# Weight work of the down projections in one chain per engine, and new orders of their units

## The chip, the core and the metric

The kernel runs on one core of a Trainium2 chip. The metric is device time in microseconds from start to end of one execution, the median of several. TensorE (PE) multiplies, VectorE (DVE) does elementwise work, ScalarE (ACT) does casts and activations, GpSimd (POOL) does a little arithmetic and some stores, and SyncE (SP) issues nearly all loads.

## What is computed

One encoder layer on 256 tokens of width 2048 in float32: two feed-forward blocks around a mixer (a gated recurrence and windowed attention). The change is in the feed-forward blocks, which run twice with other weights:

```python
def swiglu(x, w_gate_up, w_down):          # (256,2048) (2048,11264) (5632,2048)
    gate, up = jnp.split(x @ w_gate_up, 2, axis=-1)
    return (jax.nn.silu(gate) * up) @ w_down

ff = swiglu(rms_norm(x, pre_norm_ffn1[layer]), w_ffn1_gate_up[layer], w_ffn1_down[layer])
x = x + 0.5 * rms_norm(ff, post_norm_ffn1[layer])
```

## The kernel before

**Three products for one.** To keep float32 accuracy every matrix is split into a rounded part h and a remainder l (both fp32r), and a product is h·h + h·l + l·h. For weights this split is made on the fly: `split_act` casts on ScalarE (L191) and subtracts on VectorE (L192). `split_half` does it for half of a loaded tile (128x1024) and takes one of five h and one of five l buffers.

**Units.** A feed-forward block first has 11 gate-up groups of 512 columns (class `Gated`, 8 units each), then the down projection (class `Pairs`): 22 units of 256 rows of `w_down`, in two runs of 1024 output columns each. A unit's weights are 128x2048 floats, loaded in two halves of 512 KB into one of four places (`raw0` to `raw2` and a part of the tile `rooms`).

**Plain and mixed.** A plain unit (`plain`) is 8 products, 24 matmuls. A mixed unit (`seven`) uses Strassen's scheme: of the 2x2 blocks b11, b12, b21, b22 of its weights it makes sums on VectorE, and needs 7 products, 21 matmuls. Its weight work, in the order of the code: the split of b11 into ha and la; the split of the lower half (`lower`); the sum at L480 (128x1024, in place); the sums at L483 and L484 (128x512, in place); the split of the upper half (`upper`), which needs L480; the split of the lower half again (`third`), which needs L484. TensorE uses them in the order b11, lower, upper, third. The left operand of a mixed unit is a tile of sums too. For the down stages these are made once, in the gate-up stage (`units`: copy L968, sums L403 to L407, split), stored to DRAM by GpSimd (L978, tile `ss`) and read back in each run (L608, tile `sp`, 512 KB, four buffers). `MIXED` lists which of the 22 units are mixed: 0, 2, ..., 16, 20 and 21.

**The fold.** Four of the seven products add up in four banks `p` over all mixed units of a run, the rest in the four output banks `c`. When the last mixed unit and one plain unit behind it are done, `fold` (L524 to L532: one copy on ScalarE, eight additions on VectorE) adds `p` into `c`.

**Order.** Each engine runs its own queue in the order in which it was filled. That order comes from a planner at build time: it takes the instructions as traced, with priority to the earlier, and issues what its own estimate has ready. `tc.issue_after(ins)` adds a bound for it: what is traced in the block goes behind `ins` if it is on the same engine. It makes no engine wait for another. In `split_half` a bound of this kind holds splits behind `last["sums"]`, which `Gated` sets at L484 and `Pairs` does not (`AHEAD` is true there). With `AHEAD`, `seven` takes `begin_next` as `aside`: its first call loads the next plain unit's weights behind this unit's, its second splits the first half of them, between `upper` and `third`. The orders of the units in the two runs are written out by hand at L1012. In `finish` the last two units of the second run are held: their splits are made first and their products ordered by output bank, with the norm's work between.

Of the kernel before, what the change touches and what calls it, by code (L numbers as in the profile page):

```python
# [11 lines left out]
F32 = mybir.dt.float32  # L12
# [5 lines left out]
ALU = mybir.AluOpType  # L18
AX = mybir.AxisListType

P = 128
# [16 lines left out]
def hymba_layer_kernel(  # L38
# [25 lines left out]
    nc = tc.nc  # L64
# [11 lines left out]
    def nm(s):  # L76
        uid[0] += 1
        return f"{s}_{uid[0]}"

    def pa():  # L80
        return psum.tile([P, 512], F32, tag="pa", name=nm("pa"))

    def pb():
        return psum.tile([P, 512], F32, tag="pb", name=nm("pb"))
# [64 lines left out]
    def load(src, between=None):  # L149
        raw = new_raw()  # L150
        if len(src.shape) == 4:

            dst = raw.rearrange("p (a n b) -> p a n b", a=src.shape[1], n=src.shape[2])
            parts = [(dst[:, a], src[:, a]) for a in range(src.shape[1])]
        else:
            n = src.shape[1]
            dst = raw.rearrange("p (a b) -> p a b", a=n)
            parts = [(dst, src)]
            if n == 2:
                parts = [(dst[:, a], src[:, a]) for a in range(2)]  # L160
        for i, (to, of) in enumerate(parts):
            if i and between:
                between()
            nc.sync.dma_start(to, of)
        return raw

    def split_load(src, hp=hip, lp=lop, between=None, middle=None):
        return split(load(src, between), hp, lp, middle)

    def split(raw, hp=hip, lp=lop, middle=None):  # L170
        hs, ls = [], []
        for i in range(2):
            if i and middle:
                middle()
            h, l = split_half(raw, i, hp, lp)
            hs.append(h)
            ls.append(l)
        return hs, ls

    def split_half(raw, i, hp=hip, lp=lop):  # L180
        part = raw[:, i * 1024 : (i + 1) * 1024]
        h = hp.tile([P, 1024], F32R, tag="h", name=nm("h"))
        l = lp.tile([P, 1024], F32R, tag="l", name=nm("l"))
        with ExitStack() as queued:
            if "sums" in last:
                queued.enter_context(tc.issue_after(last["sums"].ins))
            split_act(h, l, part)
        return h, l

    def split_act(hi, lo, src):  # L190
        nc.scalar.copy(hi, src)  # L191
        nc.vector.tensor_tensor(lo, src, hi.bitcast(F32), ALU.subtract)  # L192


    def rsqrt_of(ssq, scale, eps):
# [17 lines left out]
    def close_far():  # L213
        far["cm"].__exit__(None, None, None)
# [15 lines left out]
    last = {}  # L230
# [114 lines left out]
    class LeadN:  # L345


        def __init__(self, w, c0, slot):
            self.w, self.c0, self.slot = w, c0, slot
# [60 lines left out]
    class Blocks:  # L410
# [1 line left out]

        AHEAD = False
        ahead = between = None

        def __init__(self, tiles, sums):
# [50 lines left out]
        def seven(self, u, aside=None):  # L469

            self.left_early(u)
            raw = load(self.source(u))
            if aside:
                aside()
            b11, b12, b21, b22 = (raw[:, i * 512 : (i + 1) * 512] for i in range(4))
            four = raw.rearrange("p (i c) -> p i c", i=4)
            h, l = self.one_block()
            split_act(h, l, b11)
            lower = split_half(raw, 1)
            nc.vector.tensor_tensor(  # L480
                four[:, 0:2], four[:, 0::3], four[:, 1:2].to_broadcast([P, 2, 512]), ALU.add
            )
            nc.vector.tensor_tensor(b22, b11, b22, ALU.add)  # L483
            sums = nc.vector.tensor_tensor(b21, b22, b21, ALU.add)  # L484
            if not self.AHEAD:
                last["sums"] = sums
            upper = split_half(raw, 0)
            if aside:
                aside()
            third = split_half(raw, 1)  # L490
            if not self.p:
                self.p = [pa(), pa(), pb(), pb()]
            a, w = self.tiles[u], self.left_sums(u)

            def lhs(k, m):
                return [a[:, k, i, m * P : (m + 1) * P] for i in range(2)]

            def summed(j):
                return [w[:, j, i, :] for i in range(2)]

            def rhs(two, n):
                return [x[:, n * 512 : (n + 1) * 512] for x in two]

            for at, left, right in (
                (("p", 0), lhs(0, 0), (h, l)),
                (("c", 0, 0), lhs(1, 0), rhs(lower, 0)),
                (("c", 0, 1), summed(S4), rhs(lower, 1)),
                (("p", 1), summed(S1), rhs(upper, 0)),
                (("p", 3), summed(S3), rhs(upper, 1)),
                (("p", 2), summed(S2), rhs(third, 1)),  # L510
                (("c", 1, 0), lhs(1, 1), rhs(third, 0)),
            ):
                self.three(at, *left, *right)
# [26 lines left out]

        def work(self, upto):

            while self.pos < upto:
                u = self.order[self.pos]
                if u in self.some:
                    v = self.order[self.pos + 1]
                    if self.AHEAD and v not in self.some and self.pos + 1 < upto:
                        self.ahead = [v]
                        self.seven(u, self.begin_next)
                    else:  # L550
                        self.seven(u)
                else:
                    if self.ahead:
                        _, raw, h, l = self.ahead
                        self.ahead = None
                        hs, ls = zip((h, l), split_half(raw, 1))
                    else:
                        hs, ls = split_load(self.source(u))
                    if self.pos == self.after + 1:
                        self.fold()  # L560
                    places = [(k, m, n) for k in range(2) for m in range(2) for n in range(2)]
                    if self.pos in (self.after, self.after + 1):

                        places.sort(key=lambda at: at[1:])
                    for i, (k, m, n) in enumerate(places):
                        if i == 4 and self.between:
                            self.between()
                            self.between = None
                        self.plain(u, hs, ls, m, n, k)
                self.pos += 1  # L570

    class Pairs(Blocks):

# [3 lines left out]
        HELD = 2  # L577
        AHEAD = True

        def __init__(self, w, orders, tiles, sums, room, gain_src, stored=False):  # L580

            super().__init__(tiles, sums)
            self.stored, self.left = stored, {}
            self.w, self.orders = w, orders
            self.room, self.post, self.gain_src = room, None, gain_src
            self.ssq = [
                stat.tile([P, 4], F32, tag="ssqr", name=nm("ssqr"), bufs=2) for _ in range(2)
            ]
            self.y = {}
            open_far(2)  # L590
            self.run(0)
# [73 lines left out]
        def finish(self, mul, post, new_x=None, gain=None, lead=None):  # L665
# [4 lines left out]
            self.post = post  # L670
            self.work(n_order - self.HELD)
            held = []
            for u in order[n_order - self.HELD :]:
                held.append((u, *split_load(self.source(u), hp=post, lp=post)))
            close_far()
            self.half_gain(post)
            raw_places[:] = [r for r in raw_places if r in own_raws]
# [172 lines left out]
    LATE = 8  # L850

    MIXED_IN = (1, 3, 5)
    MIXED = (*range(0, 18, 2), 20, 21)

    def pair_of(xt, u):
        return xt[u // 4][:, u % 4 * 2 : u % 4 * 2 + 2]
# [45 lines left out]
    def ffn(gated, w_dn, post_gain, again, gain=None, lead=None, aside=None):  # L902

        with ExitStack() as st:
# [4 lines left out]
            hts, sums = [], {}  # L909
# [33 lines left out]
            def units(c, scale):  # L943
# [19 lines left out]
                for bank in turned:  # L963
                    g = len(hts)
                    u = bank.rearrange("p (k t) -> p k t", k=2)
                    if g in MIXED:
                        u = room_for("z").rearrange("p (k t) -> p k t", k=2)
# [4 lines left out]
                    hts.append(ht)  # L972
                    if g in MIXED:
                        ws = sums_of(u, room_for("s").rearrange("p (j t) -> p j t", j=4))
# [8 lines left out]
            for g in range(NG):  # L983
# [26 lines left out]
                next(waiting)  # L1010
            close_far()
            orders = [  # L1012
                [1, 3, 0, 5, 2, 7, 4, 9, 6, 11, 8, 10, 13, 12, 15, 14, 16, 17, 20, 21, 18, 19],

                [1, 0, 3, 2, 4, 5, 6, 7, 8, 14, 9, 10, 11, 12, 16, 13, 20, 21, 15, 17, 18, 19],
            ]
            sums.update((u, None) for u in MIXED if u not in sums)
            rows = Pairs(w_dn, orders, hts, sums, work, post_gain, stored=True)
# [18 lines left out]
    with tc.manual_schedule():  # L1037
# [12 lines left out]
        def arrive(i):  # L1050
            nc.sync.dma_start(raw[:, i * 512 : (i + 1) * 512], first[:, i // 2, i % 2])

        h, l = (
            p.tile([P, 1024], F32R, tag=t, name=nm(t)) for p, t in ((hip, "h"), (lop, "l"))
        )
# [89 lines left out]
    def again_from(src):  # L1145
# [15 lines left out]
        aside=other_vectors,  # L1161
# [447 lines left out]
```

## Time and profile before

| | us |
|---|---|
| median of 3 runs | 1841.77 |
| lowest and highest | 1840.83, 1844.27 |
| the profiled execution | 1845.24 |
| its span, first to last instruction | 1843.5 |
| TensorE busy in the span | 1825.4 (99%) |
| VectorE busy | 1641.9 (89%) |
| ScalarE busy | 1106.1 (60%) |

In the profile a line number names the instruction's place in the kernel; L191 and L192 are in the helper `split_act`, so the tile's name tells whose split it is (h and l of a half, ha and la of b11, ht of the left operand). PE is TensorE's matmuls, PEld its weight loads. A row of the timeline has start, duration, engine, line, operation, output <- inputs, and in square brackets how long the engine had been idle before and what it waited for. A row of the waits has the total in us, how often, and the longest. The first down stage runs from about 488 to 702 us of the span, the second from about 1610 to 1826.

### The profile page before, as it was taken

What the parts mean: (1) busy time and instruction counts of PE and PEld (TensorE: products, weight loads), DVE (VectorE), ACT (ScalarE), POOL (GpSimd) and SP (SyncE); (2) the same over time, 40 slices, a digit from 0 to 9 for tenths busy, and PEclk for the clock granted to TensorE, in tenths of its full rate; (3) what the DMA queues carried; (4) which work ended last, traced back from release to release, by engine and by line L of the source; (5) the groups of instructions that cost most, each with busy time, mean ns of one, the idle gap of its engine ahead of it and who ended that gap; (6) DMA issues with size and microseconds to landing.
All of it is one profiled execution on the core that took longest, in us unless ns stands there. A gap on an engine that the chain in (4) does not pass through costs nothing.

```text
span 1843.5 us, 23937 instructions
## 1 busy us (share of the span) xinstructions
PE 1825.4 (99%) x8604; PEld 1519.5 (82%) x8604; DVE 1641.9 (89%) x2076; ACT 1106.1 (60%) x1470; POOL 33.2 (2%) x61
## 2 busy tenths in 40 slices
PE   9999999999999999999999999999999999999998
PEld 7888888888887787888888888888888888887786
DVE  7999999999999998477778798899999999999997
ACT  6555556555555556477678566555655555555553
POOL 1000000000000000000000000000000000000000
PEclk9999999999999999999999999999999999999999
DMA  8566666666877776655555565566666665787774
GB/s 287 195 223 219 198 196 216 215 207 207 288 264 263 239 244 212 218 179 172 163 172 165 178 223 185 197 234 212 207 218 224 212 201 194 254 275 254 244 265 169
DMA packets 192056, 400.45 MB, mean 217 GB/s; under 512 B 11976, under 2 KB 59168, under 8 KB 191168
## 3 DMA queue, kind: packets, MB, share of 16 engines
q1 hardware_dynamic: 188416, 387.24, 63.1%
q0 software_dynamic: 3520, 11.67, 1.6%
q8 instruction: 67, 1.10, 0.2%
q14 instruction: 53, 0.43, 0.1%
HBM read 383.12 MB, written 15.75 MB: 216 GB/s over the span
## 4 chain that ended last, share of the span: by engine, by line
PE 75%; DVE 14%; issue 4%; DMA 4%; ACT 3%; POOL 0%; SPq 0%; DVEq 0%; ACTq 0%; POOLq 0%
PE pa L447 29%; PE pb L447 27%; PE pa L322 8%; DVE l L192 8%; PE pa L327 4%; ACT h L191 2%; DMA raw<-in_w_mix_out_dram 1%; DMA raw<-in_w_ffn_down_dram 1%; DVE raw L480 1%; PE pa L377 1%; PE pa L376 1%; PE pa L375 1%; DVE raw L483 1%; DVE raw L484 1%; DVE la L192 1%
## 5 line engine op out<-in xcount | busy, mean ns | idle before, releaser
L191 ACT CAST h<-raw 128x1024 fp32r<-128x1024 f32 (+1 forms) x691 | 680.7, 1014 | 445.1 <-DVE raw L484 146.9
L192 DVE TENSOR_TENSOR l<-raw,h 128x1024 fp32r<-128x1024 f32 (+1 forms) x691 | 796.4, 1173 | 83.7 <-ACT h L191 43.2
L447 PE MATMUL pa<-h,xt 128*128 128x512 f32 x1176 | 406.2, 392 | 0.0
L447 PE MATMUL pb<-h,xt 128*128 128x512 f32 x1060 | 368.8, 390 | 0.0
L447 PEld LDWEIGHTS pa<-h,xt 128*128 128x128 f32 x1176 | 221.1, 188 | 45.0
L447 PEld LDWEIGHTS pb<-h,xt 128*128 128x128 f32 x1060 | 199.0, 188 | 41.3
L447 PE MATMUL pa<-l,xt 128*128 128x512 f32 x588 | 229.4, 390 | 0.1
L447 PE MATMUL pb<-l,xt 128*128 128x512 f32 x530 | 206.4, 389 | 0.0
L191 ACT CAST h<-rooms 128x1024 fp32r<-128x1024 f32 x138 | 142.3, 1049 | 86.0 <-DVE rooms L484 41.1
L192 DVE TENSOR_TENSOR l<-rooms,h 128x1024 fp32r<-128x1024 f32 x138 | 166.1, 1221 | 28.5 <-ACT h L191 28.2
L322 PE MATMUL pa<-xt,h 128*128 128x512 f32 x672 | 164.7, 394 | 0.0
L447 PE MATMUL pa<-h,ht 128*128 128x512 f32 x440 | 156.2, 391 | 2.2 <-DVE pa L526 2.1
L447 PE MATMUL pb<-h,ht 128*128 128x512 f32 x440 | 155.8, 390 | 0.4 <-DVE pb L530 0.4
L322 PEld LDWEIGHTS pa<-xt,h 128*128 128x128 f32 x672 | 123.0, 188 | 23.6
L447 PEld LDWEIGHTS pa<-l,xt 128*128 128x128 f32 x588 | 110.6, 188 | 22.8 <-DVE l L192 0.8
L447 PEld LDWEIGHTS pb<-l,xt 128*128 128x128 f32 x530 | 99.6, 188 | 20.6
L480 DVE TENSOR_TENSOR raw<-raw 128x1024 f32<-128x1024 f32 x92 | 112.1, 1219 | 1.0
L447 PEld LDWEIGHTS pa<-h,ht 128*128 128x128 f32 x440 | 82.6, 188 | 21.5 <-issue 2.8
L447 PEld LDWEIGHTS pb<-h,ht 128*128 128x128 f32 x440 | 82.6, 188 | 18.4 <-DVE pb L530 1.2
L327 PE MATMUL pa<-xt,l 128*128 128x256 f32 x672 | 91.8, 286 | 0.0
L327 PEld LDWEIGHTS pa<-xt,l 128*128 128x128 f32 x672 | 87.1, 191 | 3.2
L447 PE MATMUL pa<-l,ht 128*128 128x512 f32 x220 | 85.8, 390 | 0.0
(280 smaller groups left out, 2477.5 us busy)
## 6 DMA issues: line engine op xcount, KB each, us to landing
raw<-in_w_ffn_gate_up_dram SPq DMA_DIRECT2D x270, 512.0 KB, 5.0
raw<-in_w_ffn_down_dram SPq DMA_DIRECT2D x132, 512.0 KB, 5.4
raw<-in_w_mix_in_dram SPq DMA_DIRECT2D x52, 1024.0 KB, 4.9
rooms<-in_w_ffn_gate_up_dram SPq DMA_DIRECT2D x80, 512.0 KB, 5.1
rooms<-in_w_ffn_down_dram SPq DMA_DIRECT2D x44, 512.0 KB, 4.8
sp<-ss SPq DMA_DIRECT2D x44, 512.0 KB, 6.6
raw<-in_w_mix_out_dram SPq DMA_DIRECT2D x32, 512.0 KB, 5.3
ss<-rooms POOLq DMA_DIRECT2D x22, 512.0 KB, 3.3
```

The lines of the kernel that those rows point to most:

```text
L191: nc.scalar.copy(hi, src)
L192: nc.vector.tensor_tensor(lo, src, hi.bitcast(F32), ALU.subtract)
L322: nc.tensor.matmul(slot[f], weights(hs, kk, f), xcol(xt, k), start=(k == 0), stop=(k == KT - 1))
L327: nc.tensor.matmul(slot[f][:, 0:T], weights(ls, kk, f), xcol(xt, kh * 8 + kk, 0), start=False, stop=False,)
L375: nc.tensor.matmul(dst, xh, h[:, o : o + n], start=(k == 0), stop=False)
L376: nc.tensor.matmul(dst, xh, l[:, o : o + n], start=False, stop=False)
L377: nc.tensor.matmul(dst, xl, h[:, o : o + n], start=False, stop=(k == KT - 1))
L447: nc.tensor.matmul(self.bank(at), lhs, rhs, start=(n == 1), stop=n in (ends, self.of[at]), skip_group_check=n > ends,)
L480: nc.vector.tensor_tensor(four[:, 0:2], four[:, 0::3], four[:, 1:2].to_broadcast([P, 2, 512]), ALU.add)
L483: nc.vector.tensor_tensor(b22, b11, b22, ALU.add)
L484: sums = nc.vector.tensor_tensor(b21, b22, b21, ALU.add)
```

## The change

A function `chained` is added. While `chain["on"]` is set it places what it makes behind the last piece of chained work on VectorE and behind the last chained cast on ScalarE. `work` sets it for a `Pairs` object with stored sums, which is the case in the two down stages alone (the flag `CHAIN`), and `finish` sets it for the held splits. Every split of a weight half, the split of b11 and the three sums go through it, so that in the down stages all weight work stands on each of the two engines in the order in which it is traced. The second call of `aside` moves from between `upper` and `third` to behind `third`. Even units from 0 to 20 are mixed now: unit 18 comes in, unit 21 goes out, and there are 11 as before. The two orders of units are new. As plain (P) and mixed (M), the first run was P P M P M P M P M P M M P M P M M P M M P P and is P P M P M M P M P M M P M P M M P M P M P P; the second has P M P M M P M P M M P M P M M P M M P P P P in both.

```diff
     def split_half(raw, i, hp=hip, lp=lop):
         ...
+        if chain["on"]:
+            chained(split_act, h, l, part)
+            return h, l
         with ExitStack() as queued:
         ...
+    chain = {"on": False, "at": None}
+
+    def chained(make, *a):
+
+        with ExitStack() as queued:
+            if chain["on"]:
+                for at in ("at", "cast"):
+                    if chain.get(at):
+                        queued.enter_context(tc.issue_after(chain[at].ins))
+            chain["at"] = make(*a)
+            if make is split_act:
+                chain["cast"] = last["cast"]
+        return chain["at"]
+
     def split_act(hi, lo, src):
-        nc.scalar.copy(hi, src)
-        nc.vector.tensor_tensor(lo, src, hi.bitcast(F32), ALU.subtract)
+        last["cast"] = nc.scalar.copy(hi, src)
+        return nc.vector.tensor_tensor(lo, src, hi.bitcast(F32), ALU.subtract)
 ...
-            split_act(h, l, b11)
+            add = nc.vector.tensor_tensor
+            twice = four[:, 1:2].to_broadcast([P, 2, 512])
+            chained(split_act, h, l, b11)
             lower = split_half(raw, 1)
-            nc.vector.tensor_tensor(
-                four[:, 0:2], four[:, 0::3], four[:, 1:2].to_broadcast([P, 2, 512]), ALU.add
-            )
-            nc.vector.tensor_tensor(b22, b11, b22, ALU.add)
-            sums = nc.vector.tensor_tensor(b21, b22, b21, ALU.add)
+            chained(add, four[:, 0:2], four[:, 0::3], twice, ALU.add)
+            chained(add, b22, b11, b22, ALU.add)
+            sums = chained(add, b21, b22, b21, ALU.add)
             if not self.AHEAD:
                 last["sums"] = sums
             upper = split_half(raw, 0)
-            if aside:
+            if aside and not self.CHAIN:
                 aside()
             third = split_half(raw, 1)
+            if aside and self.CHAIN:
+                aside()
 ...
         def work(self, upto):
+            chain["on"] = self.CHAIN
             ...
+            chain["on"] = False
 ...
             self.stored, self.left = stored, {}
+            self.CHAIN = stored
 ...
+            chain["on"] = self.CHAIN
             for u in order[n_order - self.HELD :]:
                 held.append((u, *split_load(self.source(u), hp=post, lp=post)))
+            chain["on"] = False
 ...
-    MIXED = (*range(0, 18, 2), 20, 21)
+    MIXED = (*range(0, 22, 2),)
 ...
-                [1, 3, 0, 5, 2, 7, 4, 9, 6, 11, 8, 10, 13, 12, 15, 14, 16, 17, 20, 21, 18, 19],
-
-                [1, 0, 3, 2, 4, 5, 6, 7, 8, 14, 9, 10, 11, 12, 16, 13, 20, 21, 15, 17, 18, 19],
+                [1, 3, 0, 5, 2, 4, 7, 6, 9, 8, 10, 11, 12, 13, 14, 16, 15, 18, 17, 20, 19, 21],
+                [1, 0, 3, 2, 4, 5, 6, 7, 8, 10, 9, 12, 11, 14, 16, 13, 18, 20, 15, 17, 19, 21],
```

More of the change, by code (lines that the diff above doesn't have):

```diff
@@ L410, in hymba_layer_kernel @@
     class Blocks:
-        AHEAD = False
+        AHEAD = CHAIN = False
         ahead = between = None
```

## The prediction

> **What bounds the kernel now.** I read the page first, for whose time it is, then the stretches of the two down stages, then who TensorE waited for in them, and last VectorE's and ScalarE's order around the longest waits.
>
> ```profile
> span 1843.5 us, 23937 instructions
> PE 1825.4 (99%) x8604; PEld 1519.5 (82%) x8604; DVE 1641.9 (89%) x2076; ACT 1106.1 (60%) x1470; POOL 33.2 (2%) x61
> ```
>
> TensorE is the bound: it has work in 99% of the span, so only its lost starts can be won back, and the change touches the down stages alone. The stretches (busy time and count of PE, PEld, DVE, ACT, POOL, then granted clock, DMA share, GB/s) of two gate-up groups and of both down stages:
>
> ```profile
> 403.44:445.83 42.39, 42.39 (x194) 35.14 (x193) 40.40 (x47) 24.95 (x30) 0.53 (x1) 1.00 0.64 212
> 445.83:488.22 42.39, 42.39 (x192) 34.93 (x191) 38.34 (x43) 24.32 (x29) 0.00 (x0) 1.00 0.75 247
> 488.39:702.00 213.61, 210.95 (x923) 171.81 (x922) 200.85 (x221) 124.65 (x145) 1.06 (x2) 1.00 0.77 263
> 1609.66:1826.00 216.34, 212.50 (x931) 173.44 (x930) 200.42 (x220) 121.42 (x141) 1.06 (x2) 1.00 0.73 253
> ```
>
> A gate-up group has no idle PE; the down stages have 2.66 + 3.84 = 6.5 us, at full clock. That is too little, because a matmul's row is longer than its place in the stream:
>
> ```profile
> 620.64 0.39 PE L447 MATMUL pb<-h,sp 128*128 128x512 f32 x1
> 620.87 0.39 PE L447 MATMUL pb<-l,sp 128*128 128x512 f32 x1
> 621.09 0.61 PE L447 MATMUL pb<-h,sp 128*128 128x512 f32 x2
> 622.92 0.50 PE L447 MATMUL pb<-l,sp 128*128 128x512 f32 x1 [1.21 <-DVE l L192]
> 623.25 0.40 PE L447 MATMUL pb<-h,sp 128*128 128x512 f32 x1
> ```
>
> Starts are 0.227 us apart (620.64 to 621.09 is two). After the second of the pair at 621.09 (start 621.32) the next comes 1.60 later and the one behind it 0.33 later: 1.48 us lost, where the row says 1.21. Added up like this over both stages there are nine waits for an l half (first at 568.71, last at 1745.83), 6.1 us, and four waits for the fold, 4.4 us: 10.5 us in all. The rows bound it: idle weight loads from above (the waits of the weight queue in the first and then the second down stage: us, times, longest),
>
> ```profile
> PEld pb L447 <- DVE l L192: 3.4, 5, 1.6
> PEld pa L447 <- issue: 1.1, 1, 1.1
> PEld pa L447 <- DVE pa L529: 0.8, 2, 0.5
> PEld pb L447 <- DVE pb L530: 0.6, 1, 0.6
> PEld pa L447 <- DVE l L192: 0.4, 1, 0.4
> ...
> PEld pb L447 <- DVE l L192: 4.0, 4, 1.6
> PEld pa L447 <- issue: 1.7, 1, 1.7
> PEld pa L447 <- DVE pa L529: 0.8, 2, 0.5
> PEld pb L447 <- DVE pb L530: 0.6, 1, 0.6
> ```
>
> 13.4 us (7.8 for l halves, 5.6 at the folds, where I count the two "issue" rows), and the 6.5 us of idle PE from below. I take 10.5, from the starts.
>
> The Trainium skill, Perfetto Trace Analysis, Identifying the Most-Contended Engine, says that matmul busy time is a poor measure of how full TensorE is and the busy share of weight loads a good one. By that rule the loss is the fall of that share from 0.829 (35.14 of 42.39) to 0.804 and 0.802, 5.3 + 5.9 = 11.2 us; by matmul busy time it would be 6.5. The trace's starts side with the rule.
>
> **Why the l halves are late.** VectorE's order before the wait at 622.92 (the mixed unit that TensorE works on lies in "rooms", the units after it in "raw"):
>
> ```profile
> 612.74 1.22 DVE L480 TENSOR_TENSOR rooms<-rooms 128x1024 f32<-128x1024 f32 x1
> 614.03 1.23 DVE L192 TENSOR_TENSOR l<-raw,h 128x1024 fp32r<-128x1024 f32 x1
> 615.17 2.35 DVE L192 TENSOR_TENSOR l<-rooms,h 128x1024 fp32r<-128x1024 f32 x2
> 617.44 0.68 DVE L483 TENSOR_TENSOR rooms<-rooms 128x512 f32<-128x512 f32 x1
> 618.04 1.22 DVE L192 TENSOR_TENSOR l<-raw,h 128x1024 fp32r<-128x1024 f32 x1
> 619.18 0.69 DVE L484 TENSOR_TENSOR rooms<-rooms 128x512 f32<-128x512 f32 x1
> 619.78 0.68 DVE L192 TENSOR_TENSOR la<-raw,ha 128x512 fp32r<-128x512 f32 x1
> 620.50 1.23 DVE L480 TENSOR_TENSOR raw<-raw 128x1024 f32<-128x1024 f32 x1
> 621.64 1.22 DVE L192 TENSOR_TENSOR l<-rooms,h 128x1024 fp32r<-128x1024 f32 x1
> ```
>
> The third l half of "rooms" starts 8.9 us after its L480. Four pieces of other units lie between (l<-raw at 614.03 and 618.04, la and L480 at 619.78 and 620.50), some 4.1 us. VectorE isn't short of time; it does the wrong unit first.
>
> **The change, part by part.**
>
> The chain. It adds no instruction and no wait for another engine; it only fixes VectorE's and ScalarE's own order. From one 512-wide start to the next is 0.60 (617.44 to 618.04), from a 1024-wide one 1.14 (618.04 to 619.18). So VectorE pays for a mixed unit 4 x 1.14 + 3 x 0.60 = 6.3 us, for a plain one 2.3; TensorE takes 21 x 0.227 = 4.8 and 24 x 0.227 = 5.4. A run has 11 of each: VectorE 95 us, with the fold and the gains (12 x 0.60) 102, against TensorE's 112. In order, VectorE loses 1.6 us of lead in a mixed unit and wins 3.2 in a plain one. With five h and five l buffers, the second half of a plain unit takes the buffer of the plain unit before (with one mixed unit between); after that comes free, a cast and a subtraction take 2.2 us while TensorE has 4.8 + 5.4 in hand, so the lead is at most 8.0 us. Two mixed units in a row cut it to 4.8; the last third half is wanted 6 matmuls (1.4 us) before the unit's end, which leaves 3.4. No l half is late by this sum, and the 6.1 us go. Bounds: 0 won, if VectorE waits for something else, to 7.8, the weight-load rows. I take 6.0.
>
> What the chain forbids is to fill a wait with the next unit's work, and such waits exist:
>
> ```profile
> 533.23 0.69 DVE L484 TENSOR_TENSOR rooms<-rooms 128x512 f32<-128x512 f32 x1
> 535.12 1.22 DVE L192 TENSOR_TENSOR l<-rooms,h 128x1024 fp32r<-128x1024 f32 x1 [1.20 <-ACT h L191]
> ...
> DVE l L192 <- ACT h L191: 7.9, 9, 1.2
> ...
> DVE l L192 <- ACT h L191: 8.2, 8, 1.7
> ```
>
> Here the third cast can only begin after L484, and VectorE stands for it. In the chain the upper subtraction (1.14) lies in just that place, and L483 and L484 (1.2) cover the upper cast (about 1.05). I cost it at nothing; without that cover it is 1.2 us each.
>
> The fold. It isn't chained, but stands in VectorE's queue between chained work:
>
> ```profile
> 583.04 0.57 ACT L524 COPY y<-pa 128x512 f32<-128x512 f32 x1
> 585.42 0.62 ACT L191 CAST ha<-raw 128x512 fp32r<-128x512 f32 x1 [1.81 <-DMA raw<-in_w_ffn_down_dram]
> ...
> 586.07 0.69 DVE L192 TENSOR_TENSOR la<-raw,ha 128x512 fp32r<-128x512 f32 x1 [1.49 <-ACT ha L191]
> 587.02 1.23 DVE L192 TENSOR_TENSOR l<-raw,h 128x1024 fp32r<-128x1024 f32 x1 [0.26 <-ACT h L191]
> 588.16 0.69 DVE L525 TENSOR_TENSOR y<-pb,y 128x512 f32<-128x512 f32 x1
> ```
>
> L525 could run at 583.6 but stands behind a la whose weights were still on their way. In the old first run the last mixed units are two in a row; in the new one a plain unit lies between them, so VectorE is ahead by one mixed unit's loss more and frees the load's buffer some 1.6 us earlier, about as much as the transfer was late (1.81). In the second run the pattern of plain and mixed is the same as before, only the lead is larger. Bounds: nothing to 5.6; the order in the queue may stay as it is, so I take half of the 4.4, 2.2 us.
>
> The second call of aside behind the third half, and the new orders: the same casts, subtractions, loads and matmuls in other places. Each run still has 11 mixed units; the moved call issues no transfer, the next unit's load stays behind this unit's, and SyncE's loads keep the order of use. Nothing; the work that it pulls out from between the halves is late by 2 x 1.14 us for the next unit, which the lead of 4.8 covers.
>
> Unit 18 mixed in place of 21. A copy, the L403 to L407 sums, a cast, a subtraction and a 512 KB store on GpSimd's queue move from the start of the down stage into the last gate-up group. The rows above price it: a group that does this has VectorE at 40.40 of 42.39 and the DMA engines at 0.64, the last one 38.34 and 0.75, and neither has PE idle. So 2.1 us of VectorE go where another group has the same and shows no wait, and leave a place without a stall. Nothing; without that room, the 2.1 us once a stage.
>
> Sum, against the profiled execution: 1845.24 - 6.0 - 2.2 = 1837.0 (its span would be 1835.3). That execution is 3.5 us above the median, so for the median 1841.77 - 8.2 = 1833.6, say 1834.
>
> **Rivals.**
>
> Slower: bubbles in the chain. VectorE has 112 - 102 = 10 us a run to spare, 0.9 us for each mixed unit. If each has the 1.20 us wait and the 0.26 us one of 587.02, VectorE is the bound at 118 us, 5.7 a run over TensorE, four runs 23 us, and against the 10.5 lost now 12 us more: 1854. It decides from 1.27 us for each mixed unit ((10.4 + 14.2/4)/11). Against it: the order inside a mixed unit just reckoned. For it: nine and eight such waits stand there today.
>
> No change: the chain as a strict queue. Whatever waits in it for a transfer holds all behind it, the fold too, as the la at 586.07 did. If the l halves come in time but the folds lose twice what they do, 6.1 - 4.4 = 1.7 us are won: 1840. Trainium skill, TensorE: Matmul & The Clock Gate, on queue depths: ScalarE and VectorE are strict FIFOs, only TensorE pulls weight loads forward. The fold's rows agree. By that rule this rival is what any long wait in the chain comes to, about 1840.
>
> Half the gain: transfers. Two mixed units in a row take six transfers (issues in the first down stage: count, size, median us to landing),
>
> ```profile
> raw<-in_w_ffn_down_dram SPq DMA_DIRECT2D x56, 512.0 KB, 5.2
> ...
> sp<-ss SPq DMA_DIRECT2D x19, 512.0 KB, 6.5
> ```
>
> 3.15 MB in 9.5 us, 330 GB/s, where the stage moves 263: 2.4 us short of the 3.4 to spare. There are 7 such pairs a stage; if half of the 14 lose 0.6 us, 4.2 of 8.2 are given back: 1838.
>
> **How the numbers follow.** Forecast 0.57, half the gain 0.11, no change 0.17, slower 0.15. A measurement of this kernel tells some 0.2% (3.7 us) from no change, so faster is 0.68. The likeliest case alone spans 1831 (all 10.5) to 1837 (6 less a little). The range reaches down to 1829 (12.8 less, near the upper bound of the lost time, 13.4) and up to 1841.5, through most of the no-change case; the slower case is left out. 0.57 + 0.11 + most of 0.17 is about 0.8.
>
> **What would show it.** In the changed profile: VectorE in each mixed unit as la, l, L480, L483, L484, l, l; no PE row with a wait for l in the down stages; idle PE there from 6.5 to about 2; L525 within 2 us of the copy L524; gate-up groups still 42.39 us, the last at 40.4 of VectorE. Wrong, if l halves wait for casts over 1 us in most mixed units, or the L526 waits grow, or PE waits move to a DMA or an ht.

## The result, and the profile after

| | before | after |
|---|---|---|
| median, us | 1844.17 (1841.77 in the runs shown first) | 1833.25 |
| profiled execution, us | 1845.24 | 1832.80 |
| its span, us | 1843.5 | 1831.0 |

The ratio is 0.9945, with a 95% interval of 0.9932 to 0.9959: faster, by 7.5 to 12.5 us. (One run of the kernel before took twice as long as the rest and is left out, and so is one run of an experiment from its ratio.) The forecast was 1834.

Line numbers have moved: L191 and L192 are L208 and L209 now, the three sums L480, L483 and L484 all stand at L202, the products at L464, the fold at L543 to L551.

The stretches of two gate-up groups and of the two down stages, with the columns that the prediction gives for this view:

```profile
402.80:445.19 42.39, 42.39 (x195) 35.13 (x192) 40.40 (x47) 24.95 (x30) 0.53 (x1) 1.00 0.64 212
445.19:487.58 42.39, 42.39 (x195) 35.14 (x192) 39.62 (x46) 24.92 (x30) 0.53 (x1) 1.00 0.76 262
487.58:696.50 208.92, 208.92 (x924) 172.84 (x922) 203.20 (x217) 126.04 (x144) 0.53 (x1) 1.00 0.78 262
1603.00:1812.50 209.50, 209.50 (x928) 173.38 (x927) 203.44 (x217) 122.42 (x140) 0.53 (x1) 1.00 0.75 253
```

PE is busy in all of both down stages. Read by the starts of matmuls, as in the prediction, the lost time went from 10.5 us to 0.2: one start 0.11 us late in each stage. From the first product of a down stage to its last, the first stage went from 232.54 to 227.48 us and the second from 232.51 to 226.57, 11.0 us together. Of the other 1.4 us between the two profiled executions 0.8 lie ahead of the first down stage, 0.6 of it in the first 15 us, where the change does nothing. What the weight queue and VectorE still wait for in the first down stage:

```profile
PEld pa L464 <- DVE pa L548: 0.3, 1, 0.3
```

```profile
DVE l L209 <- ACT h L208: 2.6, 7, 0.8
```

VectorE waited 7.9 us for casts there before. A mixed unit is now one block on VectorE, la to la of the next unit:

```profile
603.44 0.68 DVE L209 TENSOR_TENSOR la<-raw,ha 128x512 fp32r<-128x512 f32 x1
604.04 1.22 DVE L209 TENSOR_TENSOR l<-raw,h 128x1024 fp32r<-128x1024 f32 x1
605.18 2.67 DVE L202 TENSOR_TENSOR raw<-raw 128x1024 f32<-128x1024 f32 x3
607.76 2.50 DVE L209 TENSOR_TENSOR l<-raw,h 128x1024 fp32r<-128x1024 f32 x2
610.18 0.69 DVE L209 TENSOR_TENSOR la<-rooms,ha 128x512 fp32r<-128x512 f32 x1
```

From the first sum (605.18) to the end of the last l (610.26) it is 5.1 us; before, the third l only started 8.9 us after L480. The whole block takes 6.74 us, from 603.44 to 610.18.

### The profile page after: what moved, and what is told of

The parts are those of the page before. It is cut to its first block, busy times and chain, and to the rows that moved or that the text cites. A ratio compares the mean times of both kernels' runs of the same rounds, so it can differ in the third digit from the quotient of the medians.

```text
span 1831.0 us, 23939 instructions
## 1 busy us (share of the span) xinstructions
PE 1819.6 (99%) x8604; PEld 1519.6 (83%) x8604; DVE 1649.1 (90%) x2076; ACT 1108.4 (61%) x1470; POOL 33.2 (2%) x61
## 4 chain that ended last, share of the span: by engine, by line
PE 96%; DVE 2%; DMA 1%; ACT 1%; issue 0%; SPq 0%; DVEq 0%; POOL 0%; ACTq 0%; POOLq 0%
PE pa L464 40%; PE pb L464 36%; PE pa L339 8%; PE pa L344 4%; DMA raw<-in_w_mix_out_dram 1%; PE pa L393 1%; PE pa L394 1%; PE pa L392 1%; DVE l L209 1%; PE pa L984 1%; PE pb L984 1%; PE pb L1374 0%; PE pb L1352 0%; PE pb L1436 0%; ACT xt L259 0%; ACT h L208 0%
## 5 line engine op out<-in xcount | busy, mean ns | idle before, releaser
L208 ACT CAST h<-raw 128x1024 fp32r<-128x1024 f32 (+1 forms) x693 | 685.0, 1014 | 466.8 <-DVE raw L202 267.3
L209 DVE TENSOR_TENSOR l<-raw,h 128x1024 fp32r<-128x1024 f32 (+1 forms) x693 | 798.9, 1174 | 77.7 <-ACT h L208 35.8
L464 PE MATMUL pa<-h,xt 128*128 128x512 f32 x1176 | 405.7, 391 | 0.0
L464 PE MATMUL pb<-h,xt 128*128 128x512 f32 x1060 | 368.9, 390 | 0.0
L464 PEld LDWEIGHTS pa<-h,xt 128*128 128x128 f32 x1176 | 220.9, 188 | 44.9
L202 DVE TENSOR_TENSOR raw<-raw 128x512 f32<-128x512 f32 (+1 forms) x282 | 244.6, 868 | 6.8
L464 PEld LDWEIGHTS pb<-h,xt 128*128 128x128 f32 x1060 | 198.9, 188 | 41.8 <-DVE xt L264 0.5
L464 PE MATMUL pa<-l,xt 128*128 128x512 f32 x588 | 229.5, 390 | 0.3 <-DVE l L209 0.2
L464 PE MATMUL pb<-l,xt 128*128 128x512 f32 x530 | 206.4, 389 | 0.0
L208 ACT CAST h<-rooms 128x1024 fp32r<-128x1024 f32 x136 | 140.3, 1050 | 77.6 <-PE pb L464 38.2
L209 DVE TENSOR_TENSOR l<-rooms,h 128x1024 fp32r<-128x1024 f32 x136 | 164.1, 1221 | 23.4 <-ACT h L208 22.8
L464 PE MATMUL pb<-h,ht 128*128 128x512 f32 x440 | 155.1, 389 | 0.0
L464 PE MATMUL pa<-h,ht 128*128 128x512 f32 x440 | 155.0, 390 | 0.0
L464 PEld LDWEIGHTS pa<-l,xt 128*128 128x128 f32 x588 | 110.5, 188 | 23.6 <-DVE l L209 1.6
L464 PEld LDWEIGHTS pb<-l,xt 128*128 128x128 f32 x530 | 99.5, 188 | 20.6
L464 PEld LDWEIGHTS pa<-h,ht 128*128 128x128 f32 x440 | 82.6, 188 | 17.6 <-DVE pa L548 0.5
L464 PEld LDWEIGHTS pb<-h,ht 128*128 128x128 f32 x440 | 82.6, 188 | 17.1
L464 PE MATMUL pa<-l,ht 128*128 128x512 f32 x220 | 85.6, 389 | 0.0
```

What stands on the lines that cost most here:

```text
L202: chain["at"] = make(*a)
L208: last["cast"] = nc.scalar.copy(hi, src)
L209: return nc.vector.tensor_tensor(lo, src, hi.bitcast(F32), ALU.subtract)
L464: nc.tensor.matmul(self.bank(at), lhs, rhs, start=(n == 1), stop=n in (ends, self.of[at]), skip_group_check=n > ends,)
```

## The experiments

The numbers of "lost" are sums over both down stages of a profiled execution, by the starts of matmuls; before has 10.5, after 0.2. In the shared comparisons the kernel before had medians of 1842.15 to 1842.89.

**The chain alone.** Old units, old orders.

```diff
-    MIXED = (*range(0, 22, 2),)
+    MIXED = (*range(0, 18, 2), 20, 21)
 ... both orders as before the change
```

> The chain and the moved call alone; units 20 and 21 mixed and both orders as before the change. Theory A (VectorE's order made the l halves late, and the chain mends it): no wait of TensorE for an l half is left, so 6 us of the 10.5 are won; the fold in the first run keeps two mixed units in a row ahead of it and may keep up to 3.2 us of its waits: 1834 to 1838, 0.9950 to 0.9975 of before. Rival B (the new orders and units win the time): 1840 to 1844, l halves late as before, about 6 us.

Measured: 1841.88, ratio 0.9992 (0.9983 to 1.0001): no clear gain, and the profiled execution (1839.72, among the shorter of its runs) lost 6.1 us. But the time is not lost where it was before. The nine waits for l halves and the long fold waits of the first run are gone; 5.1 of the 6.1 us are lost in one new place in each stage, 2.2 and 2.9 us some 25 us into it. Theory A held for what the chain does to the old waits and fell for the total. The total lies in rival B's range, but the late l halves by which B explained it are not there. ScalarE's timeline, and VectorE's below it, show the new wait:

```profile
496.18 1.06 ACT L208 CAST h<-raw 128x1024 fp32r<-128x1024 f32 x1
503.40 0.62 ACT L208 CAST rooms<-rooms 128x512 fp32r<-128x512 f32 x1 [6.17 <-DMA ss<-rooms]
505.97 1.04 ACT L208 CAST h<-raw 128x1024 fp32r<-128x1024 f32 x1 [1.95 <-DVE raw L202]
```

```profile
497.83 1.22 DVE L209 TENSOR_TENSOR l<-raw,h 128x1024 fp32r<-128x1024 f32 x1
504.06 0.69 DVE L209 TENSOR_TENSOR rooms<-rooms 128x512 fp32r<-128x512 f32 x1 [5.01 <-ACT rooms L208]
504.66 2.67 DVE L202 TENSOR_TENSOR raw<-raw 128x1024 f32<-128x1024 f32 x3
```

Unit 21's sums are cast into the room from which GpSimd's transfer is still storing unit 20's. ScalarE stands 6.17 us for the store, VectorE 5.01 for ScalarE, and the sums and halves of the next mixed unit stand behind both. In the kernel before, the planner had put two more weight casts ahead of this one. This cast stood for the store there too, but not as long; in the second down stage the row says so:

```profile
1622.76 0.62 ACT L191 CAST rooms<-rooms 128x512 fp32r<-128x512 f32 x1 [1.54 <-DMA ss<-rooms]
```

In the first stage the cast stood 1.45 us and began at 501.40, just behind the landing of the store at 501.3. TensorE lost nothing at either place.

**The orders and units alone.** No chain, the call of aside in its old place.

```diff
-            self.CHAIN = stored
+            self.CHAIN = False
```

> The new orders and units without the chain and with the call in its old place. Theory A: TensorE waits for l halves again, some 4 to 8 us over both down stages, with sums and halves of later units ahead of the late half on VectorE: 1837 to 1843. Rival B: as the changed kernel, 1833, no waits.

Measured: 1846.46, ratio 1.0023 (1.0014 to 1.0032), slower than before; 12.3 us lost. Theory A said that l halves would be late, but not that more would be lost than before. The longest wait, from 687.7, is not VectorE's order alone: VectorE stands for a cast, and ScalarE's queue has a cast of the next plain unit in front, which starts at 687.29 after standing 3.22 us for its load. VectorE's rows:

```profile
684.55 1.22 DVE L209 TENSOR_TENSOR l<-rooms,h 128x1024 fp32r<-128x1024 f32 x1
685.69 0.68 DVE L202 TENSOR_TENSOR raw<-raw 128x512 f32<-128x512 f32 x1
688.38 1.22 DVE L209 TENSOR_TENSOR l<-rooms,h 128x1024 fp32r<-128x1024 f32 x1 [2.01 <-ACT h L208]
```

Neither half of the change is worth much without the other: chain alone 0.9992, orders and units alone 1.0023, both 0.9945.

**Which unit's sums.** Both chains and the new pattern of plain and mixed, but 20 and 21 mixed.

```diff
-    MIXED = (*range(0, 22, 2),)
+    MIXED = (*range(0, 18, 2), 20, 21)
-   [..., 14, 16, 15, 18, 17, 20, 19, 21],   [..., 16, 13, 18, 20, 15, 17, 19, 21]
+   [..., 14, 16, 15, 20, 17, 21, 18, 19],   [..., 16, 13, 20, 21, 15, 17, 18, 19]
```

> Both chains; the new pattern of plain and mixed, but units 20 and 21 mixed as before the change, not 18 and 20. Theory D (from the run with the chain and the old orders: unit 21's sums are cast into the room from which unit 20's are still being stored, ScalarE stands 6 us for that store with the chained casts behind it, and TensorE loses 2.5 to 3 us at the start of each down stage): the same wait again, 5 to 6 us over the changed kernel, 1838 to 1842. Rival E (the pattern M M P P at the end of the first run cost it): within 0.7 us of the changed kernel, 1833.

Measured: 1839.10, ratio 0.9982 (0.9973 to 0.9991), as theory D said; 5.5 us lost, all but 0.2 of it 25 to 33 us into each stage. ScalarE again:

```profile
502.30 0.62 ACT L208 CAST rooms<-rooms 128x512 fp32r<-128x512 f32 x1 [4.23 <-DMA ss<-rooms]
```

**The pattern.** 18 and 20 mixed, the first run in the old pattern, with two mixed units ahead of the fold.

```diff
-   [1, 3, 0, 5, 2, 4, 7, 6, 9, 8, 10, 11, 12, 13, 14, 16, 15, 18, 17, 20, 19, 21],
+   [1, 3, 0, 5, 2, 7, 4, 9, 6, 11, 8, 10, 13, 12, 15, 14, 16, 17, 18, 20, 19, 21],
```

> Both chains; units 18 and 20 mixed as after the change, but the first run in the old pattern, with two mixed units in a row ahead of the fold. Theory D: no wait at the start of the down stages, nothing at the fold but tenths: within 0.7 us of the changed kernel, 1833 to 1834. Rival E: 3 to 6 us slower, 1836 to 1839, with the waits at the fold or from the old pattern.

Measured: 1834.06, ratio 0.9953 (0.9941 to 0.9966), 1.0 us lost, 0.2 of it at the first run's folds. Theory D: the units count, the pattern less than 1 us.

**A room of its own.** As in "which unit's sums", and unit 21's sums go elsewhere.

```diff
                         w = where_X_was(0).rearrange("p (j i t) -> p j i t", j=4, i=2)
+                        if g == 21:
+                            w = work.tile([P, 4, 2, P], F32, tag="sp", name=nm("w21"), bufs=3)
```

> Units 20 and 21 mixed as before the change, both chains and the new pattern, but unit 21's sums are split into a tile of their own instead of the room from which unit 20's are being stored. Theory D (the store of unit 20's sums held ScalarE's chain): the 6 us wait of that cast goes and the 5.5 us of TensorE at the start of the down stages with it: 1833.3 to 1834.5. Rival J (it is the work of a second set of sums there, 1.35 us on VectorE and 1.2 us on ScalarE, that makes the weights late): 1837 to 1839 as with the shared room.

Measured: 1833.92, ratio 0.9951 (0.9937 to 0.9965), 0.5 us lost. The cast now waits for its sums alone:

```profile
497.75 0.62 ACT L208 CAST w<-rooms 128x512 fp32r<-128x512 f32 x1 [0.71 <-DVE rooms L424]
```

All the work of the second set is still there, so it was the store and not the work: theory D is shown, rival J falls.

**One chain at a time.**

```diff
-                for at in ("at", "cast"):
+                for at in ("at",):       # VectorE alone; ("cast",) for ScalarE alone
```

> The changed kernel with VectorE's chain alone; ScalarE's casts stand as the planner puts them, which moves only the small cast ha of the next mixed unit one or two places forward. Theory A: VectorE's order is the same, a cast of 0.6 us ahead of another delays one subtraction by that, and the lead of 3 to 8 us covers it: within 0.5 us of the changed kernel, 1833. Rival C (the casts' chain is what counts): TensorE waits of several us.

> The changed kernel with ScalarE's chain alone; VectorE stands as the planner puts it. Theory A, if VectorE alone counts: late l halves where VectorE's order differs from TensorE's, 1834 to 1840. Rival C: as the changed kernel, 1833, since no subtraction can go ahead of its cast and only the sums can change places.

VectorE's chain alone: 1839.40, ratio 0.9982 (0.9973 to 0.9991), 5.1 us lost, most of it at the last mixed units and the fold of each stage's second run. Theory A said 1833; it fell. In the first down stage VectorE's weight work has the changed kernel's order, piece by piece, so these 5 us come from ScalarE's order. ScalarE's chain alone: 1835.44, ratio 0.9959 (0.9946 to 0.9973), 2.4 us lost, mostly at that same fold. That is within theory A's range and more than rival C's 1833. Here VectorE's order differs in three places of the first stage, each a sum and a subtraction of one unit changed about. So ScalarE's chain does most of the work, in part by way of VectorE: a subtraction needs its cast, and so follows the order of the casts. With VectorE's chain alone:

```profile
676.72 1.04 ACT L208 CAST h<-raw 128x1024 fp32r<-128x1024 f32 x1
680.61 1.05 ACT L208 CAST h<-rooms 128x1024 fp32r<-128x1024 f32 x1 [2.84 <-DMA rooms<-in_w_ffn_down_dram]
681.57 1.05 ACT L208 CAST h<-raw 128x1024 fp32r<-128x1024 f32 x1
```

The planner put the first cast of the next plain unit (rooms) ahead of the mixed unit's upper cast (raw). It waits for its load and then runs, the upper cast behind it, and VectorE's chain stands for that.

**How much order it takes.** The call of aside back ahead of the third split.

```diff
-            if aside and not self.CHAIN:
+            if aside:
                 aside()
             third = split_half(raw, 1)
-            if aside and self.CHAIN:
-                aside()
```

> The changed kernel with the second call of aside back between the upper and the third split, so that the chain holds the first half of the next plain unit ahead of the last l half of the mixed one. By the sum of leads (8.0 us at most, 4.8 behind two mixed units, 3.4 to spare) the 1.1 us that this costs the third half is covered: within 0.7 us of the changed kernel, 1833 to 1834. Rival F (it must be TensorE's order to the last piece): third halves late by about 1 us behind pairs of mixed units, 14 places, 5 to 14 us slower: 1838 to 1847.

Measured: 1833.44, ratio 0.9949 (0.9937 to 0.9962), nothing lost. The lead covers 1.1 us, as the sum said.

**Where the lead ends.** Six mixed units in a row in each run.

```diff
+   [1, 3, 5, 0, 7, 2, 9, 4, 11, 13, 6, 8, 10, 12, 14, 16, 15, 18, 17, 20, 19, 21],
+   [1, 0, 3, 2, 5, 4, 7, 9, 6, 8, 10, 12, 14, 16, 11, 18, 13, 20, 15, 17, 19, 21],
```

> The changed kernel with other orders: six mixed units in a row in each run, plain units before and behind. Theory A, the sum of leads: 8.7 us of lead behind two plain units, six times 1.6 and 0.15 for the short wait that the chain leaves, and the last third half wanted 1.4 us before the end: late by about 3 us, four such places, 12 us over the changed kernel: 1843 to 1848, with VectorE busy throughout. Rival H (transfers): 9.4 MB in 28.6 us is 330 GB/s where the stage moves 262, 7 us short of the same 3 to 4 to spare: 4 us at each place, 1849 or more, with VectorE and ScalarE waiting for loads. Rival I (the runs' order is free, for the five buffers and the chain are enough): 1833.

Measured: 1850.62, ratio 1.0042 (1.0029 to 1.0056); 17.3 us lost, 4.3 in each of the four blocks, where the sum said 3. What VectorE waited for most in the first stage, and the first row of the weight queue:

```profile
DVE l L209 <- ACT h L208: 9.7, 15, 1.5
```

```profile
PEld pb L464 <- ACT h L208: 4.6, 4, 1.2
```

In that stage VectorE waits for no load, so rival H has the time about right and the reason wrong. The missing 1.3 us are in the price of a mixed unit: the 6.74 us above, not 6.3 + 0.15; in the first block one la follows the other at 540.10, 546.85, 553.59 and 560.33. It then loses 2.0 of lead and not 1.75: 8.7 - 6 x 2.0 - 1.4 = -4.7, against 4.3 measured.

**Twelve mixed units.** Unit 21 mixed too, its sums in a tile of their own, `LATE = 9`, and

```diff
+   [1, 3, 0, 5, 2, 4, 7, 6, 8, 9, 10, 12, 11, 14, 16, 13, 18, 20, 15, 21, 17, 19],
+   [1, 0, 3, 2, 4, 5, 6, 8, 7, 10, 12, 9, 14, 16, 11, 18, 20, 21, 13, 15, 17, 19],
```

> The changed kernel with twelve mixed units in each run (unit 21 too, its sums in a tile of their own) and orders to suit; one left operand more is kept in the late pool. 3 matmuls of 0.227 us fewer in each of four runs are 2.7 us. Theory A: VectorE then has about 108 us of work in a run against TensorE's 111.6 and loses no more lead than it has: 1830.5 to 1832. Rival K (the second run has twelve mixed and six plain units ahead of the last four, VectorE 92 us against 90, and the loads come at 280 GB/s): waits eat it, 1833 to 1838.

Measured: 1845.41, ratio 1.0014 (1.0005 to 1.0023), 13.5 us lost: slower than rival K's range. Of K's two reasons only VectorE's work is seen, and in the runs of both stages: in the first stage VectorE waits 0.3 us in all, and for no load. Two mixed units and a plain one, over and over, on VectorE:

```profile
545.04 0.69 DVE L209 TENSOR_TENSOR la<-raw,ha 128x512 fp32r<-128x512 f32 x1
...
551.80 0.68 DVE L209 TENSOR_TENSOR la<-rooms,ha 128x512 fp32r<-128x512 f32 x1
...
558.53 2.35 DVE L209 TENSOR_TENSOR l<-raw,h 128x1024 fp32r<-128x1024 f32 x2
560.80 0.68 DVE L209 TENSOR_TENSOR la<-raw,ha 128x512 fp32r<-128x512 f32 x1
```

15.76 us for three units without a gap, where TensorE wants 2 x 4.76 + 5.44 = 14.96. VectorE has become the bound; twelve are too many for this order of work.

**The chain in the output projection too.**

```diff
-            self.CHAIN = stored
+            self.CHAIN = True
```

> The changed kernel with the chain in the mixer's output projection too. There TensorE has four waits today, at 1037.8, 1052.1, 1053.3 and 1108.6 us, 1.9 us in all with the slow matmul behind each. Theory A: VectorE's order makes them, the chain takes 1 to 1.5 us: 1831.8 to 1832.3. Rival G (the weights are not there: the projection's first loads land late): no change within 0.5 us or slower, 1833 to 1834.

Measured: 1833.13, ratio 0.9948 (0.9934 to 0.9961): no difference from the changed kernel, and theory A's 1 to 1.5 us are not won. The projection's waits sum to about 1.3 us instead of 1.9, in other places. No version tried is clearly faster than the change.

## Why the prediction was right, and where it was not

- *Where the time is lost, 10.5 us in the down stages.* Right: all but 0.2 came back. By starts of matmuls 10.5, by the share of weight loads (the Trainium skill, Perfetto Trace Analysis, Identifying the Most-Contended Engine) 11.2, by idle PE 6.5; the two stages became 11.0 us shorter.
- *The chain ends the late l halves, 6.0 us.* Right in the changed kernel. But the step reckoned with VectorE's order alone, and that is not enough: with VectorE's chain alone 5.1 us stay lost, with ScalarE's alone 2.4.
- *The fold, 2.2 of 4.4 us.* Too little: all but 0.2 us of it went. The reason given, a plain unit between the last two mixed ones, is not the cause: in the old pattern 0.2 us at the first run's folds is all that comes back, and with the new orders but no chain TensorE's weight loads still wait 2.3 us for the fold's sums in the first stage. The chain did it. The copy and the first addition of the fold in the first run:

```profile
579.99 0.58 ACT L543 COPY y<-pa 128x512 f32<-128x512 f32 x1
```

```profile
580.12 1.23 DVE L209 TENSOR_TENSOR l<-raw,h 128x1024 fp32r<-128x1024 f32 x1 [0.78 <-ACT h L208]
582.16 1.23 DVE L209 TENSOR_TENSOR l<-raw,h 128x1024 fp32r<-128x1024 f32 x1 [0.81 <-ACT h L208]
583.30 0.69 DVE L544 TENSOR_TENSOR y<-pb,y 128x512 f32<-128x512 f32 x1
```

  The addition comes 2.7 us after the copy's end, not within 2, still behind waiting splits, but TensorE doesn't wait for it. Before it was 4.5.
- *Unit 18 in place of 21: nothing.* The step that failed. It priced VectorE's time (39.62 us in the last group, 40.40 foretold) and where the store goes, and did not ask who must wait until the store has read its room. In the queues of before ScalarE did, for 1.45 and 1.54 us, and it cost TensorE nothing; in the chain it is 5.3 us of lost starts and 5.9 us of time (1839.10 against 1833.25). The total came out because the change holds both parts. For the chain alone, the same sum said 1834 to 1838 and was wrong (1841.88).
- *The sum, 8.2 us.* Too small, and that it gave the median within 1 us is in part luck: the fold's term was 2.2 us short, and the median that it was taken from, 1841.77, was 2.4 below the later 1844.17. Against the profiled execution the sum said 1837.0, and 1832.80 was measured.
- *Rival "bubbles".* The mechanism is there, at a third of its least price: 6.74 - 6.3 = 0.4 us for each mixed unit, against the 0.9 that VectorE has to spare and the 1.27 from which it decides.
- *Rival "no change", a wait in the chain holds all behind it.* Not in the changed kernel, but it is just what happened with units 20 and 21 mixed, where the cast in front waited for a store and not for a load: 0.9992 with the old orders, 0.9982 with the new. The Trainium skill, TensorE: Matmul & The Clock Gate, on engine queue depths, says that ScalarE and VectorE are strict FIFOs; those rows agree (6.17 us of ScalarE for the store, 5.01 us of VectorE behind it).
- *Rival "half the gain", transfers.* The first down stage's longest waits of VectorE and TensorE name no load, nor do they with six mixed units in a row.

## What to carry to other kernels

Where an engine has time to spare and another waits for it, look at what it does in the 5 to 10 us ahead of the wait; if it is work for later, fix the order on every engine of the chain, the one that casts as well as the one that subtracts. A fixed order then makes each wait inside it everybody's wait, so list the buffers that are written again while a transfer still reads them, and give them room or move the work; one shared room cost 5 to 6 us here, over half of the 9 us that the order won once it was out of the way (0.9951, the run with a room of its own). Count a unit's cost from a trace in which it runs in one piece, for in pieces its inner waits are filled by others.

## What the runs showed of the hardware

Sums on VectorE that each need the one before start later than others: in the changed kernel the three sums take 2.58 us from the first start to the next instruction, where the steps of 1.14 and twice 0.60 make 2.34. That is 0.24 us for two dependent steps. In the profile before, L484 directly behind the L483 that it reads from starts 0.72 us after it (532.51 and 533.23), where the step is else 0.60. Together with 0.14 us ahead of the third l half, whose cast can't begin before the last sum, it makes the 6.74 us.
